# The attention's first gate projection placed ahead of the convolution's pointwise product

## The chip, the cores and the metric

One core of a Trainium2 chip runs the whole program. The metric is the device time of one execution in microseconds (us): the median of several executions on the same chip. Before the change it is 982.55 us, the median of three runs (981.98 to 984.06).

## The reference

Two layers of a hybrid decoder trunk over 256 positions of width 2048, all in float32. Each layer normalises its input and multiplies it by one wide matrix. Three mixers read slices of the product, each is gated, and their outputs together go through an output matrix onto the residual:

```python
h = rms_norm(x, norm_w[l])
u = h @ w_in[l]
(c_in, c_gate, g_q, g_k, g_v, g_z, g_b, g_a, a_q, a_k, a_v, a_gate) = jnp.split(u, cuts, axis=-1)
y_conv = conformer_conv(c_in, ...) * jax.nn.silu(c_gate)
y_gdn = gated_deltanet(g_q, g_k, g_v, g_z, g_b, g_a, ...)
y_att = dilated_attention(a_q, a_k, a_v, cos, sin) * jax.nn.silu(a_gate)
y = jnp.concatenate([y_conv, y_gdn, y_att], axis=-1)
x = x + y @ w_out[l]
```

`conformer_conv` is a gated linear unit, a causal depthwise convolution of width 31, a LayerNorm over 512 channels, a swish, and then a pointwise product with a 512 x 512 matrix.

## The kernel before

The heavy work is a list of **projection jobs**, handed out strictly in list order by one generator, `project` (L467). A job is the product of an activation with one block of columns of a weight matrix. `HT` holds the normalised input, `YT` the gated mixer outputs, both transposed and split into a high and a low part of type fp32r, so that every product is three matmuls (high x high, low x high, high x low). A job's weights come in chunks of two 128-row blocks: SyncE's queue (SP) loads a chunk into one of four `raw` buffers (L410), ScalarE writes its high part `whi` (L432) and VectorE the low part `wlo` (L437), each into one of three buffers, and TensorE then runs the chunk's units (`unit`, L441, matmuls of L454). A job accumulates over its blocks into one of two accumulator pairs (`ACC`), and when it is done a follow-up task (`then`) empties the accumulator and gives it back.

The jobs of a layer, in order: the scalars and half of GDN's z, k, the convolution's CB and CA, q, v, the other z, the attention's q, k, v in two halves, the convolution's gate **CG** (512 columns), the pointwise product **PW** (512 columns, four 128-row blocks, `YT` as input), the attention's gate **AG** in two halves of 384 columns, and then the output projection in four or five pieces. In a job marked as channel-wise (CG, PW and AG are such) the weights are the stationary operand and 256 positions move, so a 128-row block takes three matmuls for each 128 columns.

PW reads what the convolution's task leaves: `conv_a` (L611) runs 31 steps of four operations on VectorE, then transposes (L635), sums on ScalarE, an inverse root on GpSimd (L643, L248), two normalising operations (L645), four transposes a half (L650) and the swish, which ends with the high and low parts of `YT` (L662, L663). Only then is the event `conf["pw"]` set, on which PW's units wait in the planner. `conv_gate` (L668) and `conv_out` (L677) make the gated product of PW. `att_gate(i)` (L1133) takes two buffers, scales AG's accumulator into one of them, gives it back, and makes the last rows of `YT` from the attention's output.

The order of every engine's instructions is written ahead of time by a **planner** (`Plan`, L74): each task yields operations with an engine and an estimated cost, and at each turn the operation with the earliest possible start is emitted, ties going to the lower priority number. Splits of weights have priority 0, the projection 50, `conv_gate`, `conv_out` and `att_gate` 6, the attention's head pairs 16, `conv_a` 20. On the chip each engine then runs its list in order.

The jobs around the change are these:

Of the kernel before, what the change touches and what calls it, by code (L numbers as in the profile page):

```python
# [33 lines left out]
AQ, AK, AV, AG = 4620, 5388, 6156, 6924  # L34
# [141 lines left out]
def hybrid_trunk(ctx, tc, x, x_t, w_in, conf_pw_w, w_out, params, final_norm_w, rope, lnc, out):  # L176
# [10 lines left out]
    def act(out_, in_, func=AF.Copy, scale=1.0, bias=0.0, accum=None):  # L187
        n_ap = sum(not isinstance(v, (int, float)) for v in (scale, bias)) + (accum is not None)
        kw = {} if accum is None else {"accum_out": accum}
        return ("act", 95 + _free(out_) / 1.2 + 93 * n_ap,  # L190
                lambda: nc.scalar.activation(out_, in_, func, bias=bias, scale=scale, **kw))  # L191

    def stt(out_, a, s, b, op0, op1):
        extra = 60 if not isinstance(s, (int, float)) else 0
        return ("dve", 70 + _free(out_) / 0.96 + extra,
                lambda: nc.vector.scalar_tensor_tensor(out_, a, s, b, op0=op0, op1=op1))  # L196

    def tt(out_, a, b, op):
        return ("dve", 70 + _free(out_) / 0.96, lambda: nc.vector.tensor_tensor(out_, a, b, op=op))  # L199
# [142 lines left out]
    def split(hi, lo, src, scale):  # L342

        yield act(hi, src, scale=scale)
        yield stt(lo, src, scale, hi.bitcast(F32), ALU.mult, ALU.subtract)
# [224 lines left out]
    def layer(l):  # L570
# [25 lines left out]
        def rows_scaled(dst, acc):  # L596

            yield ("wait", row_ready[l])
            yield tt(dst[:, :512].rearrange("p (a b) -> p a b", b=S), acc[0].rearrange("p (a b) -> p a b", b=S),
                     row[:, None, :].to_broadcast([128, 2, S]), ALU.mult)  # L600
            yield tt(dst[:, 512:], acc[1][:, :S], row, ALU.mult)
            yield ("put", ACC, [acc])
# [530 lines left out]
        def att_gate(i):  # L1133
            def then(acc):
                gb, th = yield ("get", S768, 2)
                yield from rows_scaled(gb, acc)
                yield act(th, gb, AF.Tanh, scale=0.5)
                yield ("wait", at_done[i])
                o = at["o", i]
                for j in range(3):  # L1140
                    s = slice(j * S, (j + 1) * S)
                    yield stt(gb[:, s], th[:, s], 1.0, gb[:, s], ALU.add, ALU.mult)
                    yield tt(gb[:, s], o[:, j], gb[:, s], ALU.mult)
                    k = 10 + 3 * i + j
                    yield from split(YT[0][:, k, :], YT[1][:, k, :], gb[:, s], 0.5)
                    yield ("set", y_ready[k])
                yield ("put", S768, [gb, th, o.rearrange("p h s -> p (h s)")])
            return then
# [100 lines left out]
        def inp(c0, n, then, prio, chan=False):  # L1249
            order = full if l or jobs else halved  # L1250
            jobs.append((HT, h_ready[l], win, c0, n, order, then, prio, None, chan))
# [12 lines left out]
            inp(AV + 384 * i, 384, heads_in(i), 7)  # L1264
        inp(CG, 512, conv_gate, 6, True)
        cs_ready = [conf["pw"]] * KB
        jobs.append((YT, cs_ready, wpw, 0, 512, full[:2], conv_out, 6, None, True))
        for i in range(2):
            inp(AG + 384 * i, 384, att_gate(i), 6, True)
        for j, (c0, n) in enumerate(pieces):  # L1270
            mode = "last" if last and j == len(pieces) - 1 else False
            jobs.append((YT, y_ready, wout, c0, n, [(4 * i, 4) for i in range(4)] if mode else full, (last_residual if last else residual)(j),
# [11 lines left out]
    for l in range(DEPTH):  # L1284
        jobs, bg = layer(l)
        all_jobs += jobs
        for gen, prio in bg:
            plan.spawn(gen, prio + 10 * l)
# [68 lines left out]
```

## Time and profile before

| what | value |
|---|---|
| median of three runs | 982.55 us |
| the profiled execution | 983.13 us, its span 981.4 us |
| TensorE (PE) busy in the span | 959.3 us, 98% |
| VectorE (DVE) busy | 758.6 us, 77% |
| ScalarE (ACT) busy | 544.7 us, 56% |
| mean granted TensorE clock | 0.991 |

The span runs from the first to the last instruction. PE is a matmul and PEld the loading of its stationary operand, which overlaps it; the ends of matmuls are modelled, so that start-to-start spacing is the surer measure. Figures in square brackets in a timeline are the idle time of the engine before the row and what ended it. Line numbers are those of the kernel, and often a helper's: L232 and L239 issue small matmuls and transposes, L454 the projection's matmuls, L191 ScalarE's operations, L196, L199, L206 and L208 VectorE's. The granted clock is a share of full speed.

### The profile page before, as it was taken

To read this page: it belongs to the slowest core of one execution; us is meant where nothing else is said; L and a number is where in the kernel's file an instruction comes from. 1 tells how busy PE (TensorE), PEld (TensorE's weight loads), DVE (VectorE), ACT (ScalarE), POOL (GpSimd) and SP (SyncE) were. 2 spreads that over 40 slices of the span, in tenths; PEclk is the share of its full clock that TensorE was granted. 3 is DMA by queue.
4 is the path that set the end of the run, shared out by engine and by line. 5 is a ranking of instruction groups with operands and counts; after the bars stand their busy time and mean duration, and the time that the engine had idled before them with its cause. 6 is when DMAs were issued, how large, how long until landed. Compare 5 with 4: busy or idle time off the path is not lost.

```text
span 981.4 us, 19748 instructions
## 1 busy us (share of the span) xinstructions
PE 959.3 (98%) x7595; PEld 937.9 (96%) x7595; DVE 758.6 (77%) x1473; ACT 544.7 (56%) x1061; POOL 57.4 (6%) x79
## 2 busy tenths in 40 slices
PE   8999999999999989999999999999999999899996
PEld 8999999999999979999899999999999999799996
DVE  7686799997999856655558768999989996666672
ACT  8764356445675665454456633564456656645551
POOL 1002000200110000000000020002001200100000
PEclk9999999999999979999999999999999999999998
DMA  9765555644445525777666555656344564467772
GB/s 335 255 215 155 184 192 181 187 145 148 150 141 186 186 65 181 223 241 222 215 200 198 197 163 172 192 179 199 124 142 152 163 201 148 131 194 222 228 251 86
DMA packets 67502, 180.31 MB, mean 184 GB/s; under 512 B 8016, under 2 KB 12240, under 8 KB 67408
## 3 DMA queue, kind: packets, MB, share of 16 engines
q1 hardware_dynamic: 64752, 174.08, 55.1%
q0 software_dynamic: 1712, 3.28, 1.3%
q10 hardware_dynamic: 944, 1.70, 0.5%
q8 instruction: 59, 0.97, 0.4%
q14 instruction: 35, 0.29, 0.1%
HBM read 173.26 MB, written 4.98 MB: 182 GB/s over the span
## 4 chain that ended last, share of the span: by engine, by line
PE 60%; DVE 1%; ACT 1%; issue 1%; ACTq 0%; POOLq 0%; POOL 0%; DVEq 0%
PE acc L454 54%; PE mix L232 3%; PE mix L239 2%; PE acc L463 1%; ACT b L191 0%; DVE b L196 0%; DVE wlo L199 0%; ACT JUNK L191 0%; ACT whi L191 0%; ACT YT L191 0%; DVE YT L199 0%; PE mix L753 0%; DVE inv L212 0%; DVE b L199 0%; ACTq L1064 0%
## 5 line engine op out<-in xcount | busy, mean ns | idle before, releaser
L454 PE MATMUL acc<-HT,whi 128*128 128x256 f32 x3072 | 541.7, 280 | 0.0
L191 ACT ACTIVATE whi<-raw 128x768 fp32r<-128x768 f32 (+4 forms) x389 | 340.1, 875 | 361.7 <-PE acc L454 311.2
L199 DVE TENSOR_TENSOR wlo<-raw,whi 128x768 fp32r<-128x768 f32 (+4 forms) x389 | 384.6, 989 | 167.1 <-ACT whi L191 163.6
L454 PEld LDWEIGHTS acc<-HT,whi 128*128 128x128 f32 x3072 | 466.4, 188 | 2.3 <-issue 1.8
L454 PE MATMUL acc<-HT,wlo 128*128 128x256 f32 x1536 | 426.7, 278 | 0.0
L454 PEld LDWEIGHTS acc<-HT,wlo 128*128 128x128 f32 x1536 | 288.6, 188 | 0.0
L454 PE MATMUL acc<-whi,YT 128*128 128x384 f32 (+2 forms) x640 | 161.8, 336 | 0.0
L196 DVE SCALAR_TENSOR_TENSOR b<-b,par,b 128x255 f32<-128x255 f32 (+20 forms) x348 | 151.9, 463 | 0.3
L454 PE MATMUL acc<-whi,HT 128*128 128x384 f32 (+1 forms) x512 | 134.6, 344 | 0.6 <-ACT whi L191 0.6
L454 PEld LDWEIGHTS acc<-whi,YT 128*128 128x128 f32 x640 | 114.0, 188 | 2.4
L454 PE MATMUL acc<-wlo,YT 128*128 128x384 f32 (+2 forms) x320 | 107.5, 336 | 0.0
L454 PEld LDWEIGHTS acc<-whi,HT 128*128 128x128 f32 x512 | 91.8, 190 | 1.3 <-ACT whi L191 1.2
L454 PE MATMUL acc<-wlo,HT 128*128 128x384 f32 (+1 forms) x256 | 87.2, 341 | 0.4 <-DVE wlo L199 0.4
L454 PEld LDWEIGHTS acc<-wlo,YT 128*128 128x128 f32 x320 | 60.1, 188 | 1.4
L454 PEld LDWEIGHTS acc<-wlo,HT 128*128 128x128 f32 x256 | 48.3, 189 | 1.1 <-DVE wlo L199 0.9
L232 PE MATMUL mix<-b,b 128*128 128x128 f32 (+5 forms) x456 | 47.3, 291 | 1.4 <-ACT b L191 1.4
L239 PE MATMUL mix<-ident,b 128*128 128x128 f32 x232 | 39.4, 290 | 7.2 <-DVE b L208 3.6
L232 PEld LDWEIGHTS mix<-b,b 128*128 128x128 f32 (+3 forms) x456 | 36.5, 163 | 8.6 <-ACT b L191 2.9
L239 PEld LDWEIGHTS mix<-ident,b 128*128 128x128 f32 x232 | 28.3, 147 | 11.2 <-DVE b L208 4.0
L191 ACT ACTIVATE b<-mix 128x384 f32<-128x384 f32 (+3 forms) x70 | 29.4, 436 | 16.9 <-PE mix L232 9.0
L196 DVE SCALAR_TENSOR_TENSOR b<-b,b 128x256 f32<-128x256 f32 (+3 forms) x62 | 31.5, 510 | 5.5 <-ACT b L191 5.4
L191 ACT ACTIVATE JUNK<-b 128x128 bf16<-128x128 f32 (+3 forms) x62 | 25.0, 403 | 16.2 <-DVE b L199 11.0
(148 smaller groups left out, 642.1 us busy)
## 6 DMA issues: line engine op xcount, KB each, us to landing
raw<-in_w_in SPq DMA_DIRECT2D x240, 384.0 KB
raw<-in_w_in SPq DMA_DIRECT2D x48, 512.0 KB
raw<-in_w_out SPq DMA_DIRECT2D x64, 384.0 KB
raw<-in_w_out SPq DMA_DIRECT2D x12, 512.0 KB
raw<-in_w_in SPq DMA_DIRECT2D x15, 396.0 KB
b<-in_x SPq DMA_DIRECT2D x10, 256.0 KB
raw<-in_conf_pw_w SPq DMA_DIRECT2D x4, 512.0 KB
raw<-in_w_out SPq DMA_DIRECT2D x8, 256.0 KB
```

Of the source, the lines that this page charges most:

```text
L191: lambda: nc.scalar.activation(out_, in_, func, bias=bias, scale=scale, **kw))
L196: lambda: nc.vector.scalar_tensor_tensor(out_, a, s, b, op0=op0, op1=op1))
L199: return ("dve", 70 + _free(out_) / 0.96, lambda: nc.vector.tensor_tensor(out_, a, b, op=op))
L232: nc.tensor.matmul(o, a, b, start=f[0], stop=f[1])
L239: nc.tensor.transpose(o, a, ident)
L454: nc.tensor.matmul(o, w, m, start=first and i == 0 and not (chan and t % 2), stop=last and i == 2, skip_group_check=chan)
L463: nc.tensor.matmul(acc[t][:, :n], YT[w][:, k, s], HT[m][:, k, :n], start=k == 0 and i == 0, stop=k == KB - 1 and i == 2)
```

## The change

The first half of the attention's gate is put into the list ahead of the pointwise product; the second half stays behind it. Nothing else is changed by hand; the planner writes its order anew from the list.

```diff
         inp(CG, 512, conv_gate, 6, True)
         cs_ready = [conf["pw"]] * KB
+        inp(AG, 384, att_gate(0), 6, True)
         jobs.append((YT, cs_ready, wpw, 0, 512, full[:2], conv_out, 6, None, True))
-        for i in range(2):
-            inp(AG + 384 * i, 384, att_gate(i), 6, True)
+        inp(AG + 384, 384, att_gate(1), 6, True)
         for j, (c0, n) in enumerate(pieces):
```

## Rows read from the trace of the kernel before

**Rows 1.** The page, part 1: TensorE's busy time in the span.

```profile
PE 959.3 (98%) x7595; PEld 937.9 (96%) x7595; DVE 758.6 (77%) x1473; ACT 544.7 (56%) x1061; POOL 57.4 (6%) x79
```

**Rows 2.** Waits of TensorE: us in total, times, longest.

```profile
PE mix L239 <- DVE b L206: 3.0, 1, 3.0
...
PE mix L232 <- ACT b L191: 1.4, 2, 1.0
```

**Rows 3.** Timeline of TensorE, layer 0: start, duration, instruction, count, idle before.

```profile
349.01 0.28 PE L454 MATMUL acc<-HT,wlo 128*128 128x256 f32 x1
352.25 0.48 PE L239 MATMUL mix<-ident,b 128*128 128x128 f32 x1 [2.97 <-DVE b L206]
353.01 2.24 PE L239 MATMUL mix<-ident,b 128*128 128x128 f32 x9 [0.28 <-ACT b L191]
355.18 1.54 PE L232 MATMUL mix<-b,b 128*64 128x256 f32 x8
356.66 1.11 PE L239 MATMUL mix<-ident,b 128*128 128x128 f32 x4
358.41 1.31 PE L454 MATMUL acc<-YT,whi 128*128 128x256 f32 x2 [0.64 <-ACT YT L191]
...
366.06 0.40 PE L454 MATMUL acc<-HT,whi 128*128 128x256 f32 x2
```

**Rows 4.** Timeline of TensorE, layer 1.

```profile
835.42 0.28 PE L454 MATMUL acc<-HT,wlo 128*128 128x256 f32 x1
...
837.87 0.33 PE L239 MATMUL mix<-ident,b 128*128 128x128 f32 x1 [2.17 <-DVE b L208]
...
843.67 0.66 PE L239 MATMUL mix<-ident,b 128*128 128x128 f32 x4
...
844.09 0.54 PE L454 MATMUL acc<-YT,whi 128*128 128x256 f32 x2
...
850.95 0.39 PE L454 MATMUL acc<-HT,whi 128*128 128x256 f32 x2
```

**Rows 5.** Windows: length, busy PE, PEld, DVE, ACT, POOL, clock, DMA share, GB/s.

```profile
349.10:366.10 17.00, 12.96 (x73) 10.56 (x72) 9.54 (x17) 10.13 (x20) 1.35 (x1) 0.70 0.17 53
835.50:850.90 15.40, 11.00 (x72) 8.87 (x72) 9.43 (x16) 10.50 (x22) 3.64 (x7) 0.89 0.41 132
366.10:399.90 33.80, 33.80 (x290) 33.80 (x289) 21.58 (x32) 15.90 (x22) 0.00 (x0) 1.00 0.58 183
850.90:883.60 32.70, 32.70 (x291) 32.70 (x291) 21.66 (x32) 16.03 (x22) 0.00 (x0) 1.00 0.59 185
...
0.00:30.00 30.00, 27.41 (x154) 26.03 (x155) 20.09 (x32) 24.28 (x56) 3.43 (x12) 1.00 0.96 342
```

**Rows 6.** The chain that ended last, in order of time: start, us, what.

```profile
359.13 59.74 PE acc L454 x443
418.88 0.66 PE mix L239 x6
```

**Rows 7.** Timeline of the convolution's tail: GpSimd and ScalarE, layers 0 and 1.

```profile
350.07 1.35 POOL L248 TENSOR_TENSOR lnst<-lnst,pw_neg 128x2 f32<-128x2 f32 x1 [74.06 <-DVE lnst L208]
...
357.72 0.63 ACT L191 ACTIVATE YT<-b 128x512 fp32r<-128x512 f32 x1 [0.49 <-DVE b L196]
...
842.83 0.63 ACT L191 ACTIVATE YT<-b 128x512 fp32r<-128x512 f32 x1 [0.38 <-DVE b L196]
```

**Rows 8.** Groups by form, ScalarE and VectorE, 366 to 400 us: busy, mean ns.

```profile
L191 ACT ACTIVATE whi<-raw 128x768 fp32r<-128x768 f32 x16 | 13.6, 847 | 18.7 <-PE acc L454 16.0 <-ACT YT L191 2.7
...
L199 DVE TENSOR_TENSOR wlo<-raw,whi 128x768 fp32r<-128x768 f32 x16 | 15.3, 958 | 12.0 <-ACT whi L191 11.9
L199 DVE TENSOR_TENSOR b<-acc,row 128x512 f32<-128x512 f32 x2 | 1.4, 692 | 0.1
```

**Rows 9.** The same view, 300 to 349 us.

```profile
L191 ACT ACTIVATE whi<-raw 128x1024 fp32r<-128x1024 f32 x10 | 10.6, 1062 | 9.4 <-PE acc L454 9.4
...
L199 DVE TENSOR_TENSOR wlo<-raw,whi 128x1024 fp32r<-128x1024 f32 x10 | 12.2, 1220 | 5.3 <-ACT whi L191 5.3
```

**Rows 10.** Instructions writing YT on VectorE: ns min/median/max, first to last start.

```profile
L199 DVE TENSOR_TENSOR YT<-b,YT x8: 681/688/693, 358.4 to 854.8; 128x512 fp32r<-128x512 f32 x8
```

## The prediction

> **What bounds the kernel now.** I read the page first. TensorE is busy 98% of the span [rows 1], so at first sight there is nothing for an order of jobs to win. But that is one mean over many stages, so I read next what TensorE waited for. Its waits are few, and the longest single one, 3.0 us, stands before a transpose that waited for VectorE [rows 2]. The timeline of TensorE shows where: in layer 0 between the gate job CG and the pointwise product PW [rows 3], and in layer 1 at the same place [rows 4]. In both, TensorE runs out of work when CG ends, because the next job needs the convolution's LayerNorm and swish, which are still being made on VectorE, ScalarE and GpSimd. What the reader is to see in [rows 3]: the last CG matmul starts at 349.01 us, then come only 22 small matmuls in four groups (1, 9, 8 and 4), the first after 2.97 us of idling, PW's first matmul at 358.41, and AG's first at 366.06.
>
> The stretches by window tell more than the idle time [rows 5]. In layer 0's stretch the granted clock is 0.70 in the mean, against 1.00 in the AG stretch behind it: with the two levels 2.4 and 1.2 GHz that is (1 - 0.70) x 2 x 17 = 10 us at 1.2 GHz. In layer 1 it is 0.89, or 3.4 us. So matmuls that count as busy ran at half speed after the idle time. Busy time hides this; I count work instead.
>
> **What the change removes.** Full-speed price: an AG stretch has 288 matmuls of 256 columns in 32.70 us in layer 1 [rows 5], 0.1135 us each. Small matmuls that stand between projection units take 0.11 us each (6 in 0.66) [rows 6]. PW is 4 blocks x 4 column tiles x 3 terms = 48 matmuls, 5.45 us; the 22 small ones are 2.42 us; together 7.87 us of work.
> Layer 0: from 349.01 + 0.11 to 366.06 are 16.94 us [rows 3]; lost 9.07. Layer 1: from 835.42 + 0.11 to 850.95 are 15.42 us [rows 4], with the same 22 and 48; lost 7.55. The sum is 16.6 us. AG's first half brings 16 x 3 x 3 = 144 matmuls, 16.3 us, that depend on nothing but the normalised input. With it between CG and PW, TensorE has 16.3 + 2.4 = 18.8 us of work while it now has 2.4.
>
> The Trainium skill (Perfetto Trace Analysis, Identifying the Most-Contended Engine) says that matmul busy time judges headroom badly, because matmuls are pipelined, and names the busy share of LDWEIGHTS in its place. By busy time the two stretches would give 4.0 + 4.4 = 8.4 us, by LDWEIGHTS 6.4 + 6.5 = 13.0 (both from [rows 5]); the rows agree with the rule in that the count above gives still more.
>
> **Is the convolution's tail ready in time?** It is not on TensorE's path if its first half is there when AG's first half ends. In layer 0 the first half is written by ScalarE at 357.72 + 0.63 [rows 7], 9.2 us after CG's end; 18.8 us are now to be had, 9.6 to spare. In layer 1 it is 842.83 + 0.63, 7.9 us after CG's end, 10.9 to spare. But the tail gets company: AG's eight weight chunks must be split while TensorE eats them, 0.85 us on ScalarE and 0.96 on VectorE each [rows 8], and the planner gives splits priority 0 and the convolution 20. ScalarE and VectorE are busy 10.1 and 9.5 us in the stretch [rows 5]; with up to seven splits more that is 16 of 18.8 us on each: it fits, with little room. If half of the splits stand in the tail's way on both engines it comes 4 x 1.8 = 7.2 us later, within the 9.6. I take that: no wait at PW. GpSimd's inverse root (1.35 us) [rows 7] stays on this tail. The bounds are 0 and 14.4 us of delay; the upper one is a rival below.
>
> **The other moves.** On the SP queue AG's first eight transfers go ahead of PW's two; POOL's queue gets nothing. A transfer stream at 0.58 of the DMA engines' time feeds AG at full speed, and 0.96 has been reached [rows 5], so the moved loads cost nothing; without that cover each chunk would cost TensorE up to its 18 matmuls, 2.04 us. PW's two splits (1.06 and 1.22 us a chunk) [rows 9] move behind AG's, beside its matmuls. The new dependence is that AG's second half takes the accumulator that AG's first half filled: two VectorE operations of at most 0.69 us [rows 8] against PW's 5.45 us, so nothing. The product's own ending has 16.3 us before the first output job instead of 32.7; now its last write starts at 854.8 in layer 1 [rows 10], 4.5 us with its own 0.69 after 850.95, so nothing. What is late next is the transposes: TensorE's order is written by the planner, and the four small groups are now set between AG's units. If the real tail is later than the planned one, all AG units behind such a transpose wait. Lower bound 0 (the small groups before CG's end are passed without idling), upper bound 3.0 a layer, the longest wait of its kind [rows 2]. I take 1.0 a layer, the longest wait on ScalarE of small matmuls set between units [rows 2], which is the nearest case: minus 2.0 us. Last, a matmul of the same form runs at two spacings: 33.80 us for layer 0's AG stretch against 32.70 [rows 5], at the same clock. Which one a stretch gets I can't tell from the order; with PW that is 1.3 us either way, taken as 0.
>
> **Sum.** 16.6 - 2.0 = 14.6 us. The profiled execution took 983.13 us (span 981.4 and 1.7 around it), 0.6 above the median of 982.55; the stretches are of that execution and nothing in them is longer for it that I can see, so I take the sum off the median: 968.0 us. Its own range: low with no waits and the faster spacing in layer 0, 982.55 - 16.6 - 1.3 = 964.6; high with 3.0 us of waits in each layer and the slower spacing in layer 1, 982.55 - 10.6 + 1.3 = 973.3.
>
> **Rivals.**
> 1. *The tail is pushed back by the splits.* For it: priorities, and 16 of 18.8 us. Against: at AG's pace VectorE still has half of each 2.04 us free. At the full 14.4 us of delay PW starts 4.8 us late in layer 0 and 3.5 in layer 1: 968.0 + 8.3 = 976.3 us. It decides from 9.6 us of delay on.
> 2. *Only the idle time comes back.* If the stretch's matmuls, packed among AG's, stay as long as they are now, the idle time alone is won, (17.00 - 12.96) + (15.40 - 11.00) = 8.4 us [rows 5]: 974.1. For it: 22 small matmuls between units may switch dearly. Against: 6 in 0.66 us were measured between units.
> 3. *The time comes back as another wait*, in the weight stream or before the output jobs: 982.5, no change. Against: in layer 0 the chain that ended last runs on TensorE's units alone for 59.74 us from PW into the output jobs [rows 6], so nothing else was late there.
> 4. *Slower.* The in-order place of the four groups, eight in all: if the planner sets each so early that it waits as long as the longest now does, 2.97 us [rows 3], 23.8 us of AG's work are held up against 16.6 won: 989.8. It decides from 2.1 us a group. For it: the tail's priority is the lowest of those at work. Against: small matmuls set between units hardly wait elsewhere [rows 2].
> That AG would not in fact run ahead of PW I give no chance: one generator hands out the projection jobs in list order.
>
> **The numbers.** Forecast 0.73, rival 1 0.09, rival 2 0.08, rival 3 0.05, rival 4 0.05. The range reaches from 964.5 over the forecast's own to 974.5, past rival 2; rivals 1, 3 and 4, 0.19 together, are left out. A difference of 0.2% (2.0 us) is about what a measurement can tell from none. Faster: 0.73 + 0.09 + 0.08 = 0.90; same 0.05; slower 0.05.
>
> **What would show it.** Right: in the profile after, AG units follow CG without a gap in both layers, the granted clock stays at 1.00 from CG to the output jobs, PW starts some 18.8 us after CG, and the way from CG's end to the first output job is shorter by some 8 us in layer 0 and 6.5 in layer 1. Wrong: a gap before PW's first matmul, waiting for YT (rival 1); idle time before L239 inside AG (rival 4); waits for whi or wlo in the AG stretch (rival 3).

## The result, and the profile after

| kernel | median, us | ratio to before (95% interval) | span of the profiled run, us |
|---|---|---|---|
| before | 983.01 (4 runs) | | 981.4 |
| changed | 969.5 (4 runs: 968.19 to 970.1) | 0.9861 [0.9844, 0.9878] | 966.4 |
| changed, in a second comparison | 968.45 (before there: 983.93) | 0.9842 [0.9828, 0.9857] | 968.2 |

The change wins 13.5 us in the first comparison and 15.5 in the second; the forecast was 14.6, to 968.0 us. The profiled execution of the changed kernel took 968.19 us, the fastest of its four, so its lengths show somewhat more than the medians do.

Where it comes from is best read as one length for each layer: from the start of CG's first matmul to the start of the first output matmul. It holds CG, PW and both halves of AG in either order. Before it is 399.99 - 320.83 = 79.16 us in layer 0 and 883.59 - 806.34 = 77.25 us in layer 1. After it is 392.14 - 321.24 = 70.90 and 868.66 - 798.51 = 70.15 us. That is 8.26 + 7.10 = 15.4 us; the spans differ by 15.0, because CG happened to start 0.4 us later. All else kept its length: between the first output matmul of layer 0 and the start of CG in layer 1 lie 406.35 us before and 406.37 after.

The page's first part shows how little the mean says, against [rows 1]: 98% before, 98% after.

```profile
PE 951.0 (98%) x7595; PEld 933.1 (97%) x7595; DVE 756.0 (78%) x1474; ACT 543.1 (56%) x1060; POOL 56.6 (6%) x79
```

The stretches by window in the changed kernel (columns as in [rows 5]): AG's first half, PW, AG's second half in layer 0, then the first two in layer 1.

```profile
349.50:368.40 18.90, 18.90 (x169) 18.46 (x168) 12.32 (x18) 14.07 (x24) 0.70 (x1) 1.00 0.58 176
368.40:375.90 7.50, 6.05 (x51) 5.66 (x50) 6.60 (x15) 3.79 (x6) 0.00 (x0) 1.00 0.35 118
...
375.90:392.10 16.20, 16.20 (x145) 16.20 (x144) 11.06 (x15) 8.14 (x11) 0.00 (x0) 1.00 0.61 191
...
827.70:846.70 19.00, 19.00 (x169) 18.56 (x168) 14.35 (x22) 14.00 (x25) 3.40 (x7) 1.00 0.72 231
846.70:852.40 5.70, 5.70 (x51) 5.58 (x50) 4.84 (x11) 2.85 (x4) 0.00 (x0) 1.00 0.49 158
```

TensorE is busy without a break for 18.90 us where it idled or ran at half speed before, and the clock is 1.00 in all five windows. The second row is the exception: of PW's 7.50 us in layer 0, 1.45 are idle. The timeline of TensorE shows the idle time, and that it is not at PW's start but in its middle (it answers to [rows 3, 4]):

```profile
349.52 0.39 PE L454 MATMUL acc<-HT,whi 128*128 128x256 f32 x2
...
364.88 0.60 PE L239 MATMUL mix<-ident,b 128*128 128x128 f32 x4
...
368.39 0.39 PE L454 MATMUL acc<-YT,whi 128*128 128x256 f32 x2
...
371.00 0.28 PE L454 MATMUL acc<-YT,wlo 128*128 128x256 f32 x1
372.10 0.38 PE L454 MATMUL acc<-YT,whi 128*128 128x256 f32 x1 [0.83 <-ACT YT L191]
373.10 0.38 PE L454 MATMUL acc<-YT,whi 128*128 128x256 f32 x1 [0.62 <-DVE YT L199]
...
375.82 0.39 PE L454 MATMUL acc<-HT,whi 128*128 128x256 f32 x2
...
846.57 0.28 PE L454 MATMUL acc<-HT,wlo 128*128 128x256 f32 x1
846.68 0.39 PE L454 MATMUL acc<-YT,whi 128*128 128x256 f32 x2
```

AG follows CG at once, the transposes for the tail's second half (364.88) are passed without idling, PW starts 18.87 us after CG as 144 + 22 matmuls at full spacing ask (18.76), and after PW's first 24 matmuls the second half of `YT` is missing. In layer 1 it is there in time. The chain that ended last tells in layer 0 what kept that half (start, us, what):

```profile
366.54 1.02 ACT whi L191
...
367.58 1.02 DVE wlo L199
...
368.73 0.68 DVE b L199
369.41 0.91 DVE wlo L199
370.32 0.34 DVE b L199
...
370.68 0.85 ACT b L191
```

These are splits of weights (`whi`, `wlo`; the first two are PW's own) and AG's gate (the two VectorE operations on `b`, and its tanh on ScalarE at 370.68), not the tail. The tail's own swish product stands on VectorE behind them, and its write of `YT` on ScalarE behind the tanh, until 371.43. The tail is one task, so the planner also sets its second half behind its first: the transposes stand at 364.88, where the low part of the first half is done at 364.3.

### The profile page after: what moved, and what is told of

Read it like the earlier page. It is cut to its first block, busy times and chain, and to the rows that moved or that the text cites. A ratio compares the mean times of both kernels' runs of the same rounds, so it can differ in the third digit from the quotient of the medians.

```text
span 966.4 us, 19748 instructions
## 1 busy us (share of the span) xinstructions
PE 951.0 (98%) x7595; PEld 933.1 (97%) x7595; DVE 756.0 (78%) x1474; ACT 543.1 (56%) x1060; POOL 56.6 (6%) x79
## 4 chain that ended last, share of the span: by engine, by line
PE 95%; DVE 1%; ACT 1%; issue 1%; DMA 1%; ACTq 0%; SPq 0%; POOLq 0%; POOL 0%; DVEq 0%
PE acc L454 85%; PE mix L232 6%; PE mix L239 3%; DMA b<-in_x_t 1%; PE acc L463 1%; DVE wlo L199 1%; ACT whi L191 0%; ACT b L191 0%; PE mix L753 0%; DVE b L196 0%; ACTq L1064 0%; ACT JUNK L191 0%; DVE b L199 0%; DVE inv L212 0%; ACTq L1063 0%
## 5 line engine op out<-in xcount | busy, mean ns | idle before, releaser
L232 PE MATMUL mix<-b,b 128*128 128x128 f32 (+5 forms) x456 | 45.5, 285 | 1.4 <-ACT b L191 1.4
L232 PEld LDWEIGHTS mix<-b,b 128*128 128x128 f32 (+3 forms) x456 | 35.7, 161 | 7.1 <-ACT b L191 2.3
L239 PE MATMUL mix<-ident,b 128*128 128x128 f32 x232 | 36.6, 275 | 0.0
L191 ACT ACTIVATE JUNK<-b 128x128 bf16<-128x128 f32 (+3 forms) x62 | 25.0, 403 | 16.1 <-DVE b L199 10.9
L191 ACT ACTIVATE b<-b,stat 128x256 f32<-128x256 f32 (+1 forms) x73 | 31.7, 450 | 1.3 <-issue 1.0
```

The lines of the kernel that those rows point to most:

```text
L232: nc.tensor.matmul(o, a, b, start=f[0], stop=f[1])
L239: nc.tensor.transpose(o, a, ident)
```

## The experiments

The theory: what TensorE lacked between CG and PW was independent work, and the loss was the time that the convolution's tail takes on the other engines; AG's first half is longer than that time and hides it. The rivals: the half-speed clock was the loss; the planner's new order as a whole made the gain; the tail's low priority was the cause, and a priority would have done the same. In the table, the two lengths are those defined above, each from two starts in the timeline (in the two kernels that hand out AG's first half ahead of CG, from the start of AG's first half).

| kernel | median, us | ratio (95%) | layer 0, us | layer 1, us |
|---|---|---|---|---|
| before | 983.0 to 983.9 | | 79.16 | 77.25 |
| changed | 969.5 | 0.9861 [0.9844, 0.9878] | 70.90 | 70.15 |
| only_layer0 | 976.53 | 0.9932 [0.9914, 0.9950] | 70.90 | 77.24 |
| only_layer1 | 975.15 | 0.9913 [0.9897, 0.9928] | 78.02 | 70.15 |
| filler | 984.97 | 1.0017 [1.0007, 1.0026] | 78.24 | 78.78 |
| third_ahead | 985.3 | 1.0024 [1.0011, 1.0037] | 76.70 | 81.46 |
| third_tail_first | 977.9 | 0.9946 [0.9929, 0.9964] | 72.85 | 77.35 |
| tail_first | 968.32 | 0.9850 [0.9834, 0.9866] | 70.61 | 70.16 |
| both_ahead | 978.07 | 0.9941 [0.9920, 0.9963] | 71.90 | 72.91 |
| ag_cg_pw | 967.2 | 0.9840 [0.9824, 0.9857] | 69.31 | 70.32 |
| tail_first_old_order | 981.59 | 0.9969 [0.9957, 0.9982] | 74.81 | 79.87 |
| ag_cg_pw_tail | 969.69 | 0.9855 [0.9839, 0.9871] | 70.36 | 71.53 |
| after_again | 968.45 | 0.9842 [0.9828, 0.9857] | 70.90 | 70.13 |

One caution for layer 0: in the profiled run of the kernel before, AG's 288 matmuls took 33.93 us from start to start there; in `only_layer1` and `filler` the same matmuls took 32.64. So 1.3 us of a difference to 79.16 can come from this alone (last section).

### One layer alone

```diff
+        if l == 0:
+            inp(AG, 384, att_gate(0), 6, True)
         jobs.append((YT, cs_ready, wpw, 0, 512, full[:2], conv_out, 6, None, True))
+        if l != 0:
+            inp(AG, 384, att_gate(0), 6, True)
```

(and the same with layer 1).

> The change made in layer 0 alone. Theory (work missing between CG and PW, a local loss): the stretch from CG's start to the first output matmul shrinks by 8.3 us as in the profile after, layer 1's stays at 77.3 us, total 974 to 976 us. Rival (the planner's whole new order made the gain, not the stretch): the total does not follow the stretch; then it may lie anywhere between 968 and 984 us.

> The change made in layer 1 alone. Theory: layer 0's stretch stays at 79.2 us, layer 1's shrinks by 7.1 us, total 975 to 977 us; the two single changes add up to the whole one within 1 us. Rival: they do not add up.

The lengths are those of the whole change where it is made, to 0.01 us, and the old one in layer 1 where it is not. The gains are 6.8 and 8.2 us by the medians (983.31 beside them), 14.9 together, against 13.5 and 15.5 for the whole change. With layer 0 alone the median is 0.5 us above the expected range; there 407.45 us instead of 406.35 lie between the two stretches, of which TensorE waits 0.81 for one split (at 793.49). The instructions of every engine stand in the same order as in the whole change but for the other layer's stretch, so the gain is local; the rival of a new order as a whole falls. One number did not fit: in only_layer1 layer 0 took 78.02 instead of 79.16 us, with nothing changed there. The last section comes back to it.

### The clock without the work

```diff
+            if w[0] is conf_pw_w:
+                for _ in range(6):
+                    yield ("pe", 975.0, lambda: [nc.tensor.matmul(acc[0][:, :S], HT[0][:, 0, :128], HT[0][:, 0, :],
+                                                                  start=True, stop=True) for _ in range(9)])
             for i, (k0, m) in enumerate(order):
```

> The kernel before, with 54 matmuls of 256 columns whose result is thrown away (they write PW's accumulator, which PW's first matmul starts anew) issued between CG and PW: 6.1 us at full speed in each layer. Theory (missing work is the loss, the lower clock only the smaller part): the granted clock stays at 1.00, PW's 48 matmuls take 5.5 instead of 7.7 us in layer 0, the small groups hurry a little; 2 to 5 us less than before, 978 to 981 us. Rival (the half-speed clock is the loss): 8 us or more less, below 975 us. Other rival (filler delays the transposes of the tail in TensorE's order): no gain or slower than 983 us.

The two stretches of layer 0 by window (CG's end to PW, then PW) and the timeline of TensorE in this run:

```profile
349.70:360.40 10.70, 9.27 (x77) 8.46 (x75) 5.78 (x12) 6.30 (x14) 1.36 (x1) 1.00 0.24 74
360.40:367.00 6.60, 6.26 (x50) 5.89 (x51) 3.67 (x5) 3.68 (x6) 0.00 (x0) 1.00 0.10 25
```

```profile
349.50 6.64 PE L496 MATMUL acc<-HT 128*128 128x256 f32 x54
355.99 1.25 PE L239 MATMUL mix<-ident,b 128*128 128x128 f32 x10
...
360.40 0.38 PE L454 MATMUL acc<-YT,whi 128*128 128x256 f32 x1 [1.43 <-ACT YT L191]
```

The clock stayed at 1.00, as both sides expected, and the time did not fall: 984.97, slower by 0.17%. PW with its own wait took 366.82 - 360.40 = 6.42 us against 7.65 before [rows 3], so the clock gave back 1.2 us there (0.2 in layer 1, 6.70 against 6.86). But the 54 matmuls went as one block ahead of the small matmuls of the tail, which had begun 3.1 us after CG's end and now begin 6.5 us after it; PW started 10.9 us after CG's end instead of 9.3. The third expectation was the right one. With the clock restored, PW still waits for the tail.

This run moved the transposes too, so it alone can't tell what the clock cost ahead of PW. `only_layer1` can: its layer 0 has every engine's instructions in the order of the kernel before, but a higher clock between CG and PW. The windows from CG's end to PW's first matmul, before and in `only_layer1`, and that matmul:

```profile
349.10:358.40 9.30, 5.42 (x24) 3.31 (x22) 5.98 (x13) 6.50 (x15) 1.35 (x1) 0.64 0.25 85
...
349.50:358.80 9.30, 4.58 (x25) 2.95 (x23) 5.98 (x13) 6.50 (x14) 1.35 (x1) 0.82 0.27 85
...
358.76 0.38 PE L454 MATMUL acc<-YT,whi 128*128 128x256 f32 x1 [1.32 <-ACT YT L191]
```

At 0.64 that is (1 - 0.64) x 2 x 9.3 = 6.7 us at 1.2 GHz, at 0.82 it is 3.3, and PW starts 9.29 us after CG's end in both; TensorE only idles longer. So half of the time at 1.2 GHz ahead of PW could go without PW starting any sooner, because the tail sets that time; inside PW the clock cost 1.2 us. The rival that it was most of the loss falls.

### A third of the cover

```diff
-        for i in range(2):
-            inp(AG + 384 * i, 384, att_gate(i), 6, True)
+        inp(AG, 128, att_gate(0, 0, 1), 6, True)
         jobs.append((YT, cs_ready, wpw, 0, 512, full[:2], conv_out, 6, None, True))
+        inp(AG + 128, 256, att_gate(0, 1, 3), 6, True)
+        inp(AG + 384, 384, att_gate(1), 6, True)
```

(The blocks of the weights are laid out to match, and `att_gate` takes the range of its 128-column pieces.)

> Only a third of AG's first half (128 columns, 48 matmuls, 5.45 us) stands between CG and PW; the other 256 columns follow PW. Theory (each us of independent work wins a us up to what the tail needs): about 5.5 us in each layer, 9 to 12 us in all, 971 to 974 us, with a wait of 1 to 4 us left before PW. Rival (any cover that keeps the clock up is enough): as much as the whole change, 968 to 970 us.

A miss: 985.3 us, no gain at all, and slower than before in layer 1. My reading that each microsecond of work wins a microsecond is wrong. TensorE had its 48 matmuls more, but waited for PW all the same, 4.44 us in layer 0:

```profile
357.69 0.28 PE L455 MATMUL acc<-HT,wlo 128*128 128x256 f32 x1
...
358.70 0.66 PE L240 MATMUL mix<-ident,b 128*128 128x128 f32 x4
363.79 0.38 PE L455 MATMUL acc<-YT,whi 128*128 128x256 f32 x1 [4.44 <-ACT YT L192]
```

ScalarE's list says why (lines are one higher in this kernel):

```profile
357.25 1.01 ACT L192 ACTIVATE b<-mix,par 128x256 f32<-128x256 f32 x2
359.23 1.06 ACT L192 ACTIVATE whi<-raw 128x1024 fp32r<-128x1024 f32 x1 [0.97 <-DMA raw<-in_conf_pw_w]
360.19 0.40 ACT L192 ACTIVATE b<-b 128x256 f32<-128x256 f32 x1
360.50 0.61 ACT L192 ACTIVATE whi<-raw 128x512 fp32r<-128x512 f32 x1
361.01 0.61 ACT L192 ACTIVATE b<-b 128x512 f32<-128x512 f32 x1
363.11 0.94 ACT L192 ACTIVATE YT<-b 128x512 fp32r<-128x512 f32 x2 [1.48 <-DVE b L197]
```

The first row and the last two are the tail. Between them stand PW's split, waiting 0.97 us for its weights, the gate's tanh of the moved third, and a split for the job behind PW. Counted from CG's start, the first half of `YT` was begun 41.12 us later here (363.11 - 321.99) and 36.89 before (357.72 [rows 7] - 320.83): 4.2 us of delay for a cover of 5.45 us. In layer 1 the delay is 5.6 us (847.14 - 805.05 against 842.83 - 806.34), and PW's 48 matmuls take 10.44 us instead of 6.86, with 1.73 us of waiting for the low part of `YT` and a granted clock of 0.67. So what is moved ahead brings its own work on ScalarE and VectorE and shifts the jobs behind it, and these splits, with their waits for weights, go ahead of the tail. That layer 0 is 2.5 us shorter is the cover less the delay, 1.2, and AG's spacing, 1.3.

### The tail first

The same third, and the whole change, with the tail as a task of its own:

```diff
             yield ("put", S1024, [cx])
+            plan.spawn(conv_tail(ca), -1)
+
+        def conv_tail(ca):
             sm = small([128, 4 * NT], f"lnst{l}")
```

> The kernel with only a third of AG's half ahead of PW, which gained nothing, and the tail at priority -1. Theory (that cover bought nothing because its splits and its gate pushed the tail back by as much as it covered): the waits before PW fall from 4.4 us in layer 0 and 5.2 in layer 1 to 2 us or less each, 974 to 979 us. Rival (the tail is long by itself, or the 128-column chunks are what costs): 983 to 986 us as before.

> The changed kernel with the convolution's tail (from its first transposes on) as a task of its own at priority -1, ahead of the splits (0), the gates (6) and the attention (16). Theory (in the changed kernel the tail is late because splits and gates go first on VectorE and ScalarE): the second half of YT comes several us earlier than 22.5 us after CG's end in layer 0, the 1.5 us of waiting inside PW go, 967 to 968.5 us against 969.5. Rival (the tail's own chain sets its end): no difference, 969 to 970 us. Other rival (now splits are late): TensorE waits for whi or wlo in AG, 971 us or more.

With a third as cover, priority turns no gain into 5.3 us (977.9): the wait before PW falls from 4.44 to 0.61 us in layer 0. That the work in the lists had pushed the tail back is shown by this pair there. In layer 1 the expectation missed: the two waits at PW fall from 3.47 + 1.73 to 1.97 + 0.77 us, not to 2 or less, and the length, 77.35 us, is that of the kernel before. There ScalarE waits for the weights of the moved third itself, and TensorE 1.56 us for their split:

```profile
836.65 0.42 ACT L192 ACTIVATE whi<-raw 128x256 fp32r<-128x256 f32 x1 [2.73 <-DMA raw<-in_w_in]
```

The kernel before and the changed one have no such wait for a load on ScalarE in these stretches, so in layer 1 a part of the third's failure lies in its small chunks and their late loads, as the rival had it; how large a part no run shows.

With the whole change, the second half of `YT` begins on ScalarE at 359.64 instead of 371.43, and both waits inside PW are gone, as expected:

```profile
359.64 0.62 ACT L191 ACTIVATE YT<-b 128x512 fp32r<-128x512 f32 x1
```

PW is 1.78 us shorter (5.65 against 7.43). But layer 0's length falls by 0.29 us only, because CG and AG's first half take 48.0 us (321.41 to 369.41) against 47.2 and AG's second half 16.96 against 16.32, with no wait in them; 968.3 us can't be told from 969.5 and 968.45.

### Both halves ahead

```diff
+        inp(AG, 384, att_gate(0), 6, True)
+        inp(AG + 384, 384, att_gate(1), 6, True)
         jobs.append((YT, cs_ready, wpw, 0, 512, full[:2], conv_out, 6, None, True))
```

> Both halves of AG ahead of PW. Theory: the wait inside PW goes (1.5 us less in layer 0), but now the product's ending (two VectorE and then a ScalarE and a VectorE operation, some 2.7 us) stands between PW and the first output job, so TensorE waits 2 to 4 us there in each layer; 971 to 975 us. Rival (more cover is better): 968 us. Which means that the amount that is moved has an optimum at one half.

The wait is where it was expected, before the first output matmul, and has the expected size, 2.82 us; but the time is 978.07, above the expected 971 to 975. The timeline of TensorE, and the windows of the wait and what follows, show the rest:

```profile
390.29 0.28 PE L454 MATMUL acc<-YT,wlo 128*128 128x256 f32 x1
393.39 0.69 PE L454 MATMUL acc<-whi,YT 128*128 128x384 f32 x1 [2.82 <-ACT YT L191]
394.29 0.69 PE L454 MATMUL acc<-whi,YT 128*128 128x384 f32 x1 [0.22 <-DVE YT L199]
```

```profile
390.30:392.60 2.30, 0.27 (x3) 0.07 (x1) 2.30 (x5) 0.61 (x2) 0.00 (x0) 0.99 0.74 208
392.60:399.40 6.80, 5.80 (x17) 5.40 (x18) 3.49 (x8) 2.51 (x5) 0.00 (x0) 0.50 0.50 165
399.40:410.00 10.60, 10.60 (x63) 10.60 (x62) 4.27 (x6) 4.24 (x5) 0.00 (x0) 1.00 0.53 154
```

After the idle time the clock is 1.2 GHz for 6.8 us, and the output jobs of layer 0 take 94.52 us (393.39 to 487.91) against 91.36 in the changed kernel (392.14 to 483.50). So here a wait of 2.8 us cost 3.2 us more behind it. In layer 1 the same wait of 2.82 us stands there, and from the first output matmul to the end of the span it is 100.3 us against 97.7. This was not in the expectation. Dense work stands behind this wait; behind the old one stood small matmuls that waited for the tail anyway.

### Another order, and priority alone

`ag_cg_pw` hands out AG's first half ahead of CG too, so that CG is the cover; `ag_cg_pw_tail` adds the tail's priority to it; `tail_first_old_order` has the priority with the jobs as before.

```diff
+        inp(AG, 384, att_gate(0), 6, True)
         inp(CG, 512, conv_gate, 6, True)
         cs_ready = [conf["pw"]] * KB
-        inp(AG, 384, att_gate(0), 6, True)
```

> AG's first half ahead of CG as well, so that CG covers the tail. Theory (any independent job of the length will do, and the later conv_gate work no longer stands in the tail's way on VectorE and ScalarE): no wait before or in PW, 967 to 969 us. Rival (the gate's late work delays the product's ending, or buffers run short): 970 us or more.

> The order AG's first half, CG, PW with the tail at priority -1 as well. Theory (in that order nothing waits before or in PW any more, so the tail's priority has nothing left to give): as AG, CG, PW alone, within 1 us of 967.2. Rival (the two add): 966 us or less.

> The kernel before, in its old order of jobs, with only the convolution's tail at priority -1. Theory (a part of the old gap is the tail queueing behind other work, the rest its own length): with the tail first the half that PW needs comes some 5 us sooner after CG's end in layer 0 (3.8 us in the run that has both, 9.2 before) and hardly sooner in layer 1 (10.1 against 7.1 there); 977 to 981 us. Rival (priority alone would have done what the change did): 970 us or less. Other rival (the tail is only its own length): no difference, 982 to 984 us.

> The changed kernel as it is, once more, beside the two others on one chip: 969 to 970 us, so that the difference to AG, CG, PW (967.2) is read on the same runs.

In `ag_cg_pw` the last 19.3 us ahead of PW, now filled by CG, and PW's own matmuls have no idle time, so another independent job of that length does as well:

```profile
349.30:368.60 19.30, 19.30 (x172) 18.86 (x171) 13.06 (x20) 14.90 (x28) 0.80 (x1) 1.00 0.45 143
368.60:374.00 5.40, 5.40 (x50) 5.40 (x49) 4.21 (x6) 2.60 (x4) 0.00 (x0) 1.00 0.47 147
```

Its ratio, 0.9840, can't be told apart from the changed kernel's, 0.9861 and 0.9842 (the repeat took 968.45 us, a little under the 969 to 970 expected). The priority adds nothing to it: 969.69 us is outside the expected 1 us around 967.2, and its ratio, 0.9855, is again not to be told apart. Alone, in the old order, the priority gives 0.3%, 981.59 us, just above the expected 977 to 981: 4.4 us less in layer 0 and 2.6 more in layer 1, of which AG's spacing is 1.3 each time (32.64 instead of 33.93, and 33.92 instead of 32.64). In layer 0 the first half of `YT` is begun at 353.34, 3.2 us after the transposes behind CG begin at 350.12, and TensorE still does not start PW:

```profile
350.12 0.93 PE L239 MATMUL mix<-ident,b 128*128 128x128 f32 x7
352.12 0.55 PE L239 MATMUL mix<-ident,b 128*128 128x128 f32 x3 [1.07 <-ACT b L191]
353.83 2.11 PE L232 MATMUL mix<-b,b 128*64 128x256 f32 x8 [1.17 <-DVE b L212]
355.87 1.12 PE L239 MATMUL mix<-ident,b 128*128 128x128 f32 x4
356.64 0.78 PE L454 MATMUL acc<-YT,whi 128*128 128x256 f32 x2
```

The waits are now those of the attention's last head pair (L232 behind a VectorE copy), which stands in TensorE's list ahead of PW. Two short chains shared layer 0's gap; a priority shortens one, independent work covers both.

## Why the prediction was right

**The lost time.** Counted as work at full spacing, 9.07 and 7.55 us were lost. The stretch became shorter by 8.26 and 7.10, with the waits below still in it. In layer 0 PW took 375.82 - 368.39 = 7.43 us instead of 5.45, 1.98 lost; against that AG's second half ran at the faster spacing (288 matmuls took 33.93 us from start to start before, 1.2 more than at 0.1135 each, which was not in the 9.07), and the cover took 0.1 more than its work. 9.07 + 1.2 - 1.98 - 0.1 = 8.2. In layer 1 PW took 5.66 and the cover 18.98 us, 0.4 us above their work: 7.55 - 0.4 = 7.1. So the counting held. The Trainium skill (Perfetto Trace Analysis, Identifying the Most-Contended Engine) names the busy share of LDWEIGHTS as a measure of headroom, next to the share of peak work. By that share 13.0 us were to be had, nearer to the 15.4 measured than the 8.4 of matmul busy time; the trace agrees with the rule so far. It is still short, since slower weight loads count as busy too: 72 took 10.56 us in layer 0's stretch, 0.147 each, against 0.112 in the AG stretch of layer 1 (291 in 32.70) [rows 5].

**The waits.** Near in sum, wrong in place, and the nearness is luck: 2.0 us were taken off for transposes, and some 2.5 were lost elsewhere (1.98 + 0.1 in layer 0, 0.4 in layer 1), against which the faster spacing, taken as 0, gave 1.2 back. I wrote "What is late next is the transposes" and took 1.0 us a layer there. No transpose was waited for in either layer. Late was the tail's second half, in layer 0 alone, with 1.45 us of idle time inside PW. I had checked only "if its first half is there". That half came 362.65 + 0.61 - 349.5 = 13.8 us after CG's end, 4.6 later than before, within the 9.6 I allowed and near the 7.2 I took. The second came 22.5 us after it, 10.3 later than before (360.68 + 0.63 - 349.1 = 12.2): 4.6 of these it has from the first half, on which it follows, and 5.7 are its own, behind splits and AG's gate. `tail_first` showed it: with the tail ahead of these the two waits are gone.

**The splits in the tail's way** (rival 1) were the right danger. At the full cover they cost little, as 16.3 us are more than the tail plus its delay; in `third_ahead` they and late weights took most of what the cover gave in layer 0 and more than that in layer 1. The prediction had them fit "with little room": they did for the first half of the tail, and not for the second half in layer 0.

**The rest.** The moved loads, the accumulator's hand-over and the product's ending cost nothing in the changed kernel, as said; `third_ahead` shows loads that come late, and `both_ahead` the ending's price when its cover goes. That the clock would stay at 1.00 from CG to the output jobs came true. Rival 2 (only idle time comes back, 974.1) and rival 4 (slower by transposes placed too early) did not occur in the changed kernel. That matmuls placed in TensorE's list can hold up others is real, but the case seen is the reverse of rival 4: in `filler` matmuls without use held up the transposes.

## What to carry to other kernels

Where the bound engine waits for a chain on other engines, look for an independent job that is already in the list and put it before the wait; but count that job's own work on the engines of the chain, and its loads. A cover shorter than the chain plus that delay can win nothing (a third of it: 0.2% slower), and taking more than is needed can uncover the next chain (both halves: 978 instead of 969 us). Price such a stretch by its matmuls times their spacing at full clock, not by idle time.

## What the hardware showed that was not expected

A matmul of one form runs at two spacings at the same granted clock, and the order of instructions does not settle which. Layer 0's AG stretch of 288 matmuls took 33.80 us before [rows 5]; in `only_layer1`, whose layer 0 is the same instruction for instruction on every engine, it took

```profile
366.60:399.20 32.60, 32.60 (x291) 32.60 (x289) 21.56 (x32) 15.94 (x22) 0.00 (x0) 1.00 0.61 186
```

From start to start that is 33.93 against 32.64 us, 1.29 less, and more than the whole 1.14 us by which its unchanged layer was shorter; PW took 0.15 longer, and the shorter spell at 1.2 GHz gave nothing. Runs of such a kernel can differ by a microsecond or more for this alone; what sets the spacing stays open.
